# Key and value products under the list scheduler, with norm chains shared by two tiles

## The chip, the cores and the metric

The kernel runs on one core of a Trainium2 chip. The metric is device time in microseconds of one launch, as the median of several runs; the profile is one more execution with the hardware profiler on. Differences of about 0.2% (3.2 us) can be told from no change.

## The reference, cut to what matters

Two layers over x (1024 tokens, 1024 features), all in float32. Layer A is attention over a window of 128 tokens, with 16 query heads on 4 key/value heads of 64; layer B has three branches (compressed, selected and sliding window) on one shared key/value side.

```python
def swa_layer(x, ...):                     # layer A
    proj = rms_norm(x, norm_g) @ w_in      # columns: queries 1024, keys 256, values 256, gates z 1024
    q = rms_norm(q, q_gain); k = rms_norm(k, k_gain)      # per head of 64
    o = banded_attention(q, k, v, SWA_WINDOW, table, sink)
    return x + (o * silu(z)) @ w_out

def nsa_shared_kv(x, ...):                 # once, from layer A's output
    kv = rms_norm(x, norm_g) @ w_kv        # six parts of 256: cmp k, cmp v, slc k, slc v, win k, win v
    k_cmp = rms_norm(compress(kv[:, :, 0], ...), k_gain[0]); v_cmp = compress(kv[:, :, 1], ...)
    k_slc = rms_norm(kv[:, :, 2], k_gain[1]); v_slc = kv[:, :, 3]
    k_win = rms_norm(kv[:, :, 4], k_gain[2]); v_win = kv[:, :, 5]

def nsa_layer(x, ...):                     # layer B
    proj = rms_norm(x, norm_g) @ w_in      # queries 1024, branch gates 48, three gates z of 1024
    # three attentions, gated by z and the branch gates, summed, @ w_out, + x
```

`compress` takes overlapping blocks of 32 tokens (stride 16), adds a position embedding and sends each block of 32 x 64 numbers through two products with a SiLU between.

## The kernel before, in words

**Products.** The 1024 tokens are eight tiles of 128. Each float32 operand is split in a high part (rounded to TensorE's float32 format, cast by ScalarE) and a low part (the rest, a subtraction on VectorE), and a product is three: high x high, high x low, low x high. A product of a token tile with 512 columns is thus 8 x 3 matmuls (`proj_steps`, lines 291 to 293). For it the tile's rows are scaled with their norm (L333 or L335), turned on TensorE in two groups of four 128x128 blocks (L341), and split into the tensor `xt` (L228, L229).

**Norms without a square root.** The inverse root is a chain of twelve small VectorE operations (`rsqrt_steps`, L197 to L214), each on the result of the last. Each row norm of x needs one per tile, and each key tile one for its heads (`head_steps`): copy of the keys (ScalarE, L497), square (GpSimd, L447), sum (VectorE, L451), chain, product with the root (GpSimd, L465), turn (TensorE, L476), split (L231, L232), store.

**Weights.** `load_w` loads 512 KB at a time into one of two stages and splits it into a slot. Slots are a ring of seven: four in the pool `w`, three in `wx`. `preload` takes all four of `w` for weights of the attention stage, and what comes after it in the program runs on the three of `wx`.

**The order.** In layer A's keys (`layer_a`) the steps of tile i stand in lists (load, statistics and scale, turns, product, chain, turn of the keys), and `weave` interleaves the lists of successive tiles by position; the result is the order of the engines' queues (`manual_schedule`). `shared_kv` does the same with `pipeline`: first the normed rows and the first half of layer B's keys (`kv_units`, tile `bkv`), then the products for the compressed keys and values (tile `c`) and the turns of their tokens (L1216), then the compression (`hid_ck`, `hid_cv`), then the second half of the keys. Queries and gates (`query_chunk`, `z_half`) stand outside of such a region, and the framework orders them itself around it; it also fits whole regions into one another, but keeps each one's own order on every engine.

The two attention stages (`plan_a`, `plan_b`) are ordered by the class `Plan`, a list scheduler. Every operation is entered with its engine, a cost, what it comes after, the ring buffers that it opens and uses, a priority and a latency; a load also holds a modelled DMA for a time. `Plan.run` then always picks the ready operation that can start earliest,

```python
key = (max(at, free.get(e, 0.0)) + o["shy"], o["prio"], o["n"])
```

and emits it; ties go to the lower priority number. The costs are written into the program; the chip's own times don't enter.

**Gates.** Layer A's gates z (`z_half`, tile `z_a`) follow its queries: the four key loads of two halves each (`load_keys`, 512 KB each, from DRAM), then four branches of weights `az`; at branch 1 `preload` comes first. A gate's store is issued by ScalarE itself. Layer B has twelve such branches, in the order c = 0 to 3 and, inside, b = 0 to 2; there `preload` comes ahead of branch (2, 0).

## Time and profile before

| | us |
|---|---|
| median of three runs | 1600.13 (1598.68 to 1600.6) |
| the profiled execution | 1605.16 |
| its span, first to last instruction | 1603.4 |
| mean granted TensorE clock | 0.979 |

The times of the trace are microseconds from the start of the span. Layer A's keys and values are made up to about 95 us, its queries to 190, its gates to 254, its attention and output to 485; layer B's keys and compressed keys take 498 to 693, its queries to 794, its gates to 965, its attention and output the rest. PE is TensorE, DVE VectorE, ACT ScalarE, POOL GpSimd and SP SyncE, whose only work is to issue loads and stores; a q behind a name means the engine's sequencer. A clock of 0.5 is 1.2 GHz, 1.0 is 2.4 GHz.

### The profile page before, as it was taken

The numbers are of one execution on the slowest core, as the hardware profiler recorded it, in microseconds if no ns is written. First come the engines' busy times: TensorE is split into PE (matmuls) and PEld (weight loads), VectorE is DVE, ScalarE is ACT, GpSimd is POOL, SyncE is SP. The second block draws the span as 40 slices with busy tenths as digits, with TensorE's granted clock in tenths as the row PEclk, the third lists the DMA queues.
The fourth block names the chain that finished last, engine by engine and source line by source line (L and its number), as shares of the span: only waits on it lengthen the run. The fifth ranks groups of instructions, "written<-read, shape, count | busy, mean of one in ns | idle before, by whom it ended". The sixth has DMA issues, their size and how long they took to land.

```text
span 1603.4 us, 26419 instructions
## 1 busy us (share of the span) xinstructions
PE 1518.9 (95%) x8579; PEld 1206.2 (75%) x8579; DVE 981.1 (61%) x4051; ACT 786.1 (49%) x1895; POOL 344.2 (21%) x442
## 2 busy tenths in 40 slices
PE   5899998989996989999999999999999999989998
PEld 3678876767774868899888787777787787768777
DVE  6668723766535645589732434877787787576531
ACT  4323323765633334233332433877677777675530
POOL 2124300112000100133300000332333343354300
PEclk8999999999997989999999999999999999999999
DMA  5265486554325323365553443435423433363132
GB/s 188 68 178 147 128 224 184 158 185 141 103 83 180 103 76 95 111 168 130 147 148 109 131 125 112 127 86 142 115 83 117 146 99 102 112 193 91 42 114 93
DMA packets 199692, 203.89 MB, mean 127 GB/s; under 512 B 22159, under 2 KB 160098, under 8 KB 199556
## 3 DMA queue, kind: packets, MB, share of 16 engines
q1 hardware_dynamic: 177552, 189.50, 40.7%
q10 hardware_dynamic: 21124, 10.49, 2.3%
q0 software_dynamic: 880, 2.23, 0.6%
q8 instruction: 68, 1.11, 0.3%
q14 instruction: 68, 0.56, 0.1%
HBM read 147.41 MB, written 56.85 MB: 127 GB/s over the span
## 4 chain that ended last, share of the span: by engine, by line
PE 61%; DVE 4%; DMA 2%; issue 1%; ACT 1%; POOL 1%; SPq 0%; POOLq 0%; DVEq 0%; ACTq 0%
PE o_b L857 7%; PE pt_sb L848 4%; PE s_sb L1381 4%; PE z_b L320 3%; PE z_b L321 3%; PE z_b L322 3%; PE s_wb L1381 3%; PE pt_wb L848 3%; PE z_b L619 2%; PE bq L291 2%; PE bq L292 2%; PE bq L293 2%; PE z_b L620 2%; PE z_b L621 2%; PE op L759 2%; PE op L760 2%
## 5 line engine op out<-in xcount | busy, mean ns | idle before, releaser
L910 ACT ACTIVATE p_sb<-p_sb,negm_sb 128x128 f32<-128x128 f32 (+7 forms) x128 | 98.8, 774 | 10.8 <-DVE negm_sb L1418 10.1
L910 ACT ACTIVATE p_wb<-p_wb,negm_wb 128x640 f32<-128x640 f32 (+4 forms) x128 | 88.7, 695 | 22.1 <-DVE negm_wb L1418 21.3
L320 PE MATMUL z_b<-xt_b,w_bz 128*128 128x512 f32 x240 | 95.1, 398 | 3.9 <-ACT w_bz L231 3.9
L852 ACT COPY p_sb<-pt_sb 128x512 f32<-128x512 f32 x143 | 78.2, 587 | 41.9 <-PE pt_sb L848 41.5
L1381 PE MATMUL s_sb<-k,q_b 128*128 128x384 f32 (+3 forms) x384 | 96.5, 368 | 2.1 <-DVE mx_sb L1409 1.7
L321 PE MATMUL z_b<-xt_b,w_bz 128*128 128x512 f32 x240 | 94.9, 395 | 0.0
L322 PE MATMUL z_b<-xt_b,w_bz 128*128 128x512 f32 x240 | 94.8, 395 | 0.0
L568 DVE SCALAR_TENSOR_TENSOR zt_b<-zt_b,z_b 128x512 f32<-128x512 f32 x48 | 32.8, 686 | 98.1 <-ACT zt_b L565 98.0
L1381 PE MATMUL s_wb<-k,q_b 128*128 128x384 f32 (+3 forms) x384 | 85.8, 334 | 2.4 <-issue 1.7
L852 ACT COPY p_wb<-pt_wb 128x512 f32<-128x512 f32 x120 | 67.9, 583 | 36.7 <-PE pt_wb L848 35.8
L900 POOL TENSOR_TENSOR uz_b<-uz_b,rb_b 128x512 f32<-128x512 f32 x32 | 42.1, 1316 | 190.9 <-DMA rb_b<-rdb 158.2
L848 PE MATMUL pt_sb<-consts,p_sb 128*128 128x128 f32 x576 | 79.8, 276 | 1.2 <-ACT p_sb L852 0.7
L848 PEld LDWEIGHTS pt_sb<-consts,p_sb 128*128 128x128 f32 x576 | 65.4, 140 | 17.2 <-issue 10.0
L565 ACT ACTIVATE zt_b<-z_b 128x512 f32<-128x512 f32 x48 | 28.5, 596 | 96.9 <-PE z_b L322 76.4
L910 ACT ACTIVATE p_a<-p_a,negm_a 128x256 f32<-128x256 f32 (+1 forms) x128 | 61.7, 483 | 27.8 <-DVE negm_a L1109 19.9
L770 DVE TENSOR_TENSOR xo<-op,xo 128x512 f32<-128x512 f32 x32 | 22.1, 690 | 86.3 <-PE op L761 86.2
L900 POOL TENSOR_TENSOR uz_a<-uz_a,rb_a 128x256 f32<-128x256 f32 x32 | 25.0, 782 | 222.7 <-DMA rb_a<-rda 199.8
L857 PE MATMUL o_b<-p_sb,v 128*64 128x256 f32 x576 | 72.8, 391 | 0.0
L1400 DVE CUSTOM_DVE_ANT_1 p_sb<-s_sb,sel_b 128x256 f32<-128x256 f32 (+3 forms) x128 | 56.6, 453 | 25.7 <-PE s_sb L1381 21.7
L848 PE MATMUL pt_wb<-consts,p_wb 128*128 128x128 f32 x480 | 71.1, 275 | 0.1
L1558 POOL TENSOR_TENSOR pc_b<-pc_b,mxc_b 128x256 f32<-128x256 f32 x32 | 20.7, 647 | 233.1 <-DVE mxc_b L1555 186.4
L1381 PEld LDWEIGHTS s_sb<-k,q_b 128*128 128x128 f32 x384 | 62.6, 191 | 9.9 <-issue 2.9
(386 smaller groups left out, 4605.1 us busy)
## 6 DMA issues: line engine op xcount, KB each, us to landing
ws_bz<-in_b_w_in_dram SPq DMA_DIRECT2D x24, 512.0 KB
uz_b<-uzb SPq DMA_DIRECT2D x32, 384.0 KB
qda<-qs_aq SPq DMA_DIRECT2D x64, 128.0 KB
q_a<-qda SPq DMA_DIRECT2D x32, 256.0 KB
qdb<-qs_bq SPq DMA_DIRECT2D x64, 128.0 KB
q_b<-qdb SPq DMA_DIRECT2D x32, 256.0 KB
rb_b<-rdb SPq DMA_DIRECT2D x64, 128.0 KB
uzb<-zt_b ACTq DMA_DIRECT2D x30, 256.0 KB
```

What stands on the lines that cost most here:

```text
L291: mm(ps, xh, w(0, k), start=(k == 0), stop=False)
L320: mm(ps, wh, xh, start=(k == 0), stop=False)
L321: mm(ps, wl, xh, start=False, stop=False)
L322: mm(ps, wh, xl, start=False, stop=(k == KC - 1))
L568: nc.vector.scalar_tensor_tensor(c["t"], c["t"], 1.0, ps(), op0=ALU.add, op1=ALU.mult)
L848: nc.tensor.transpose(t[:, g * P : (g + 1) * P], p()[:, g, cols], self.ident)
L852: nc.scalar.copy(p()[:, :, cols], t) if e == "ACT" else nc.vector.tensor_copy(p()[:, :, cols], t)
L857: nc.tensor.matmul(o()[z * HD : (z + 1) * HD], v()[:, blocks[j], :], p()[:, z::2, j * P : (j + 1) * P], start=(j == 0), stop=(j == n - 1),)
L900: nc.gpsimd.tensor_tensor(u(), u(), c["b"], op=ALU.mult)
L910: self.nc.scalar.activation(p[:, g, :n], p[:, g, :n], AF.Exp, bias=negm[:, g : g + 1], accum_out=sums[:, g : g + 1])
L1381: nc.tensor.matmul(s["s"][:, : nbk * P], cq(g), k[:, y, (b0 + at) * P : (b0 + at + nbk) * P], start=(y == 0), stop=(y == 1),)
L1400: nc.vector.tensor_tensor_reduce(out, src, term, 1.0, NEG, ALU.add, ALU.max, acc)
```

## The change

The keys and values of layer A, and all of `shared_kv`, are entered into a `Plan` instead of lists. One plan covers layer A's loads of x, weights, norms, turns, products and keys, and the weights of the first queries. A second one covers layer B's keys, the compression and the weights of the first queries there (`w3`). Row norms of layer A share a chain in groups (0), (1), (2, 3), (4, 5), (6, 7); keys share copy buffer, square, sum, chain, turn, split and store by two tiles. In layer A rows 4 to 7 of x and two weight stages use the memory of the bias tables `dd`, and all low parts of the key weights are VectorE's (half of them were GpSimd's). Queries turn and split up to 512 columns at once. In layer A's gates SyncE keeps the program's order, and the key loads come after the last branch's weights, their first 256 columns for all heads ahead of the rest. In layer B the preload comes one branch earlier.

```diff
+    def plan_rsqrt(self, get, n, scale, name, c, after, new, use, prio):
+
+        for k, step in enumerate(self.rsqrt_steps(get, n, scale, name, c)):
+            after = [self.plan.op("DVE", 0.19, step, after, [] if k else new, use + (new if k else []), prio, 0.02)]
+        return after[0]
...
+    def plan_weights(self, w, c0, n, name, prio, gain=None, rows=D, stage=None, own=None, early=None):
...
+            part = m * n / SLOT
+            pr = prio[j] if isinstance(prio, list) else prio + 0.01 * j
+            a = plan.op("SP", 0.5, load, [], stgs, [], pr if early is None else early + 0.01 * j, 2.5, held=2.0 * part)
+            a = plan.op("ACT", part if gain is None else 0.15 * m + 0.9 * part, high, [a], ws, stgs, pr)
+            b = plan.op("DVE", 1.22 * part if gain is None else 0.1 * m + 1.25 * part, low, [a], [], stgs + ws, pr)
...
+    def plan_proj(self, c, xt, i, weights, xops, name, prio, parted=False, first=()):
...
+        if parted:
+            order = [(k, (0,)) for k in (0, 1, 2, 3)] + [(0, (1,)), (1, (1,)), (4, (0,)), (5, (0,)), (2, (1,)), (3, (1,))]
+            order += [(6, (0,)), (7, (0,))] + [(k, (1,)) for k in (4, 5, 6, 7)]
+        else:
+            order = [(k, (0, 1)) for k in range(KC)]
+        a, steps = None, []
+        for n, (k, ys) in enumerate(order):
+            need = [made[k][0] if 0 in ys else None, made[k][1] if 1 in ys else None]
+            a = plan.op(
+                "PE", 0.227 * (2 * (0 in ys) + (1 in ys)), run(k, ys, n == 0, n == len(order) - 1),
+                [a] + need + xops[k // 4] + (list(first) if n == 0 else []), [] if n else [mb],
+                bufs[k] + ([mb] if n else []), prio, 0.35 if n == len(order) - 1 else 0.0,
+            )
...
+    def plan_norm(self, c, j, x, after, xt, i, name, prio, gain=None, xbuf=()):
...
+        a = plan.op("DVE", 1.31 if gain else 0.72, scale, after, [], ([chain] if chain else []) + list(xbuf), prio)
...
+            t = plan.op("PE", 0.66, turn, [a], [tb], list(xbuf), prio + 0.1 * k)
+            b = plan.op("ACT", 0.57, high, [t], [], [tb], prio + 0.1 * k)
+            b = plan.op("DVE", 0.66, low, [b], [], [tb], prio + 0.1 * k)
...
+    def plan_keys(self, pool, cs, bufs, ready, kd, gain, m, name, prio, gop=None):
...
+        rs = [plan.op("ACT", 0.36, raw(0), [ready[0]], [kb], [bufs[0]], prio)]
+        rs.append(plan.op("ACT", 0.36, raw(1), [ready[1]] + rs, [], [kb, bufs[1]], prio))
+        a = plan.op("POOL", 1.08, square, rs, [sb], [kb], prio)
+        a = plan.op("DVE", 0.66, reduce, [a], [cb], [sb], prio)
+        a = self.plan_rsqrt(lambda: c["hs"], 8, 1.0 / HD, nm, c, [a], [], [cb], prio)
+        a = plan.op("POOL", 1.06, normed, [a], [nb], [kb, cb], prio)
+        a = plan.op("PE", 0.66, turn, [a], [tb], [nb], prio)
+        a = plan.op("ACT", 0.57, high, [a, gop], [qb], [tb], prio)
+        a = plan.op("DVE", 0.68, low, [a], [], [tb, qb], prio)
+        plan.op("SP", 0.5, store, [a], [], [qb], prio, 2.2, held=1.46)
...
# layer_a
+                plan_load(0, -100)
+                iop = plan.op("SP", 0.4, ident, [], [], [], -99, 2.2, held=0.3)
+                plan_load(1, -98)
...
+                wkv = self.plan_weights(
+                    w_in, 1024, 512, "akv", [-11.0, -4.0, -3.5, -3.0], stage=lambda j: places[j] if j >= 2 else None, early=-97.0
+                )
...
+                for i in range(2, NT):
+                    plan_load(i, 10.0 * i - 80)
+                waq = self.plan_weights(w_in, 0, 512, "aq0", 55.0)
...
+                for tiles in ((0,), (1,), (2, 3), (4, 5), (6, 7)):
+                    i0 = tiles[0]
+                    cb = plan.buf("chain")
+                    c = {"buf": cb}
+                    prio = 10.0 * i0 - 22
...
-            for h in range(NKV):
-                self.load_keys(ks[h], kd, h, 0, S)
-            for c in range(4):
-                if c == 1:
-                    self.preload(w_in, [1536 + (self.zfirst + k) * 256 for k in range(2)], None)
-                    self.lasting = 0
-                w = self.load_w(w_in, 1536 + c * 256, 256, f"az{c}")
...
+            with tc.manual_schedule(engines={mybir.EngineType.SP}):
+                for c in range(4):
+                    if c == 1:
+                        self.preload(w_in, [1536 + (self.zfirst + k) * 256 for k in range(2)], None)
+                        self.turn = self.lasting = 0
+                    w = self.load_w(w_in, 1536 + c * 256, 256, f"az{c}")
+                    if c == 3:
+                        for k0, k1 in ((0, 256), (256, S)):
+                            for h in range(NKV):
+                                self.load_keys(ks[h], kd, h, k0, k1)
...
# shared_kv
+            ld = plan.op("SP", 0.45, load, [], [xb], [], 10.0 * i - 99, 2.3, held=1.9)
+            xops[i] = self.plan_norm(c, 0, lambda c=c: c["x"], [ld], xt, i, "kv", 10.0 * i - 15, None, [xb])
...
+        branch(0, self.plan_weights(kw, 512, 512, "bkv0", -5.0, gain, early=-98.0), 0.0)
+        wc = self.plan_weights(kw, 0, 512, "ckv", 50.0, gain)
+        sw = plan.op("SP", 0.0, swap, [x for i in range(NT) for y in xops[i] for x in y], [], [], -100.0, 0.0)
...
+            steps, mb = self.plan_proj(c, xt, i, wc, xops[i], f"c_{i}", 100.0 + 10.0 * i)
+            for z, ops in enumerate(self.plan_tokens(p1, c, mb, [steps[-1], sw], es, i, 105.0 + 10.0 * i)):
+                tokens[z] += ops
...
+        branch(1, (wkv, made0 + made1, bufs0 + bufs1), 240.0, [rv["last"]])
+        w3 = self.plan_weights(w_in, 3 * 256, 304, "bq3", 290.0, lambda: self.gb)
...
# build
-                    if (c, b) == (2, 0):
+                    if (c, b) == (1, 2):
                         self.preload(w_in, [1072 + k * D + self.zfirst * 256 for k in range(2)], self.gb)
-                        self.lasting = 0
+                        self.turn = self.lasting = 0
```

## Rows read from the trace of the kernel before

**Rows 1.** The page's part 1, TensorE's line: busy us (share of the span) xinstructions.

```profile
PE 1518.9 (95%) x8579; PEld 1206.2 (75%) x8579; DVE 981.1 (61%) x4051; ACT 786.1 (49%) x1895; POOL 344.2 (21%) x442
```

**Rows 2.** The table by stretches: start:end, length, then busy time of each engine in each of these stretches of the span (us from its start), with the number of instructions, the granted TensorE clock, the DMA share and GB/s. In order: the keys of layer A (two stretches), its gates, the end of its attention and the step into layer B, the first keys of layer B, the token products for the compressed keys, the queries of layer B, and its gates.

```profile
10.00:35.00 25.00, 13.89 (x53) 10.30 (x52) 18.04 (x47) 11.90 (x18) 6.35 (x3) 0.83 0.60 200
...
35.00:89.00 54.00, 45.66 (x204) 35.44 (x203) 35.29 (x164) 17.92 (x36) 10.84 (x13) 0.92 0.18 56
...
190.00:254.00 64.00, 58.33 (x253) 47.14 (x251) 22.41 (x45) 16.11 (x25) 3.13 (x3) 0.95 0.82 221
...
462.00:500.00 38.00, 24.97 (x108) 20.18 (x107) 15.79 (x56) 9.45 (x20) 0.00 (x0) 0.83 0.41 140
...
500.00:553.00 53.00, 51.53 (x249) 41.25 (x248) 37.75 (x119) 20.49 (x42) 7.68 (x13) 0.96 0.48 139
...
553.00:625.00 72.00, 62.35 (x291) 49.22 (x289) 34.98 (x82) 26.00 (x55) 2.06 (x4) 0.93 0.24 71
...
693.00:794.00 101.00, 101.00 (x636) 92.12 (x635) 88.00 (x374) 35.51 (x87) 36.03 (x48) 1.00 0.58 145
...
794.00:980.00 186.00, 182.09 (x794) 149.35 (x793) 67.67 (x157) 60.49 (x133) 3.13 (x3) 0.98 0.46 129
```

**Rows 3.** The same table for seven shorter stretches, the columns as in rows 2.

```profile
23.10:26.70 3.60, 3.57 (x11) 2.92 (x12) 0.86 (x1) 1.53 (x2) 0.00 (x0) 0.51 0.56 212
...
34.30:40.30 6.00, 5.99 (x16) 4.86 (x17) 2.82 (x22) 0.59 (x1) 0.00 (x0) 0.50 0.00 0
...
54.00:57.40 3.40, 3.40 (x11) 2.71 (x12) 1.99 (x14) 0.82 (x3) 0.00 (x0) 0.50 0.00 0
...
244.40:248.50 4.10, 4.05 (x10) 3.19 (x11) 1.82 (x2) 0.49 (x1) 0.00 (x0) 0.50 0.91 286
...
498.50:504.50 6.00, 6.00 (x19) 4.76 (x20) 1.95 (x3) 1.17 (x2) 0.00 (x0) 0.50 0.58 232
...
570.50:576.20 5.70, 5.70 (x17) 4.75 (x18) 2.37 (x4) 2.04 (x4) 0.00 (x0) 0.50 0.32 83
...
898.30:903.90 5.60, 5.60 (x13) 4.45 (x14) 3.33 (x8) 2.97 (x8) 0.00 (x0) 0.50 0.71 187
```

**Rows 4.** The view of TensorE's waits, asked for one stretch of the span after another (0 to 89, 89 to 190, 190 to 254, 462 to 553, 553 to 625, 794 to 990 us): who waited <- for whom: us in total, times, longest us.

```profile
PE xt_a L341 <- DVE x L333: 21.7, 8, 7.2
...
PE qt_aq L476 <- DVE ks_a L232: 1.8, 1, 1.8
...
PE z_a L320 <- ACT w_az L228: 5.1, 1, 5.1
...
PE xt_kv L341 <- DVE xk L335: 13.0, 1, 13.0
...
PE kt_b L476 <- POOL qn_b L465: 6.8, 2, 6.1
...
PE z_b L320 <- ACT w_bz L231: 3.9, 1, 3.9
```

**Rows 5.** VectorE in the keys of layer A. First two rows of the timeline (start us, us, engine, line, operation, out<-in), the first and the last of the twelve operations of tile 0's chain; then rows of the groups by form of 0 to 90 us (line, engine, operation, shapes xcount | busy us, mean ns | idle before).

```profile
5.43 0.15 DVE L197 TENSOR_SCALAR rx_a<-ss_a 128x1 f32<-128x1 f32 x1 [3.90 <-ACT jk_a L360]
...
7.55 0.16 DVE L214 SCALAR_TENSOR_TENSOR ry_a<-rt_a,ry_a 128x1 f32<-128x1 f32 x1
...
L333 DVE SCALAR_TENSOR_TENSOR x<-x,rsa,gain 128x1024 f32<-128x1024 f32 x8 | 10.9, 1362 | 0.6 <-DVE rsa L363 0.3
...
L229 DVE TENSOR_TENSOR xt_a<-xt_a,xt_a 128x512 fp32r<-128x512 f32 x16 | 11.0, 690 | 14.9 <-ACT xt_a L228 14.9
...
L229 DVE TENSOR_TENSOR w_aq<-ws_aq,w_aq 128x1024 fp32r<-128x1024 f32 x4 | 4.9, 1228 | 3.0 <-ACT w_aq L228 3.0
...
L232 DVE SCALAR_TENSOR_TENSOR ks_a<-kt_a,cols,ks_a 128x256 fp32r<-128x256 f32 x5 | 2.4, 484 | 2.5 <-ACT ks_a L231 2.5
```

**Rows 6.** TensorE's timeline at the first transposes of tiles 1, 6 and 7 of layer A; in brackets its idle time before, and what ended it.

```profile
23.13 1.09 PE L341 MATMUL xt_a<-consts,x 128*128 128x128 f32 x4 [7.16 <-DVE x L333]
...
72.74 0.63 PE L341 MATMUL xt_a<-consts,x 128*128 128x128 f32 x4 [2.02 <-DVE x L333]
...
81.07 0.63 PE L341 MATMUL xt_a<-consts,x 128*128 128x128 f32 x4 [1.44 <-DVE x L333]
```

**Rows 7.** The end of layer A's gates: SyncE's timeline at the key loads, ScalarE's at the last cast of gate weights, and the table by stretches (columns as in rows 2) from 230 to 234 us.

```profile
218.78 7.00 SPq L515 DMA_DIRECT2D k_a<-kda  x8
...
243.35 1.04 ACT L228 CAST w_az<-ws_az 128x1024 fp32r<-128x1024 f32 x1 [4.46 <-DMA ws_az<-in_a_w_in_dram]
...
230.00:234.00 4.00, 4.00 (x20) 3.30 (x19) 0.00 (x0) 0.00 (x0) 0.00 (x0) 1.00 1.07 257
```

**Rows 8.** The step into layer B: timeline of ScalarE, SyncE and VectorE.

```profile
486.92 2.54 ACT L231 ACTIVATE w_bkv<-ws_bkv,cols 128x512 fp32r<-128x512 f32 x4
...
490.16 1.85 SPq L259 DMA_DIRECT2D ws_bkv<-in_kv_w_dram  x2
...
492.06 2.11 SPq L1234 DMA_DIRECT2D xk<-x1d  x4
...
497.60 0.75 DVE L335 TENSOR_SCALAR xk<-xk,r 128x1024 f32<-128x1024 f32 x1 [1.55 <-DMA xk<-x1d]
```

**Rows 9.** GpSimd's timeline at the key norm of the last tile of layer B's first keys.

```profile
569.81 0.61 POOL L465 TENSOR_TENSOR qn_b<-kr_b,ry_b 128x256 f32<-128x256 f32 x1 [5.96 <-DVE ry_b L214]
```

**Rows 10.** ScalarE's timeline in layer B's gates, at a part of the preloaded weights.

```profile
891.75 1.71 ACT L231 ACTIVATE w_pre<-ws_pre,cols 128x256 fp32r<-128x256 f32 x4 [2.17 <-PE z_b L322]
```

More of the change, by code (lines that the diff above doesn't have):

```diff
@@ L242, in slot, with load_w @@
         return self.wx.tile([P, 2, SLOT], F32R, tag="wx", name=name, bufs=self.wmore)
-    def load_w(self, w, c0, n, name, gain=None, rows=D, later=None, stage=None, low=None):
+    def load_w(self, w, c0, n, name, gain=None, rows=D):
         kk = SLOT // n
@@ L984, in layer_a @@
                 nc.vector.memset(one, 1.0)
-                square, *chain = units[0][1]
-                square()
-                for z in range(2):
-                    cols = slice(z * 512, (z + 1) * 512)
-                    ps_g = self.mm(f"gain_{z}")
-                    nc.tensor.matmul(ps_g, one, row[z], start=True, stop=True)
-                    nc.scalar.copy(gain[:, cols], ps_g)
-                turn = units[0][2]
-                for step in (*chain, later[0], turn[0], later[1], turn[1], later[2], later[3], *units[1][1]):
-                    step()
@@ L995, in layer_a, with ident @@
[L995 to L1004 removed]
+                def ident():
+                    nc.sync.dma_start(table[:, :P], a["consts"][:, :P])
@@ new lines, in masks, with gain_row, run, gain_copy @@
+                def masks():
+                    nc.sync.dma_start(table[:, P:], a["consts"][:, P:])
+                gc = {}
+                def gain_row(z):
+                    def run():
+                        gc[z] = self.mm(f"gain_{z}")
+                        nc.tensor.matmul(gc[z], one, row[z], start=True, stop=True)
+                    return run
+                def gain_copy(z):
+                    return lambda: nc.scalar.copy(gain[:, z * 512 : (z + 1) * 512], gc[z])
+                xs, loads = {}, {}
@@ new lines, in plan_compress @@
+        tb = plan.buf("tp")
+        a = plan.op("PE", 0.1, turn, [ld], [tb], [], prio - 30)
+        z = plan.op("DVE", 0.17, clear, [tokens[0]], [], [], prio - 30)
+        a = plan.op("ACT", 0.2, high, [a, z], [], [tb], prio - 30)
+        a = plan.op("DVE", 0.2, low, [a], [], [tb], prio - 30)
+        w, made, bufs = self.plan_weights(w1, 0, 256, f"{name}w", prio - 20, rows=2048)
+        pb = [plan.buf("mm") for _ in range(2)]
+        after = [a] + tokens
+        for k in range(16):
+            a = plan.op(
+                "PE", 0.74, product(k), after + list(made[k]), [] if k else pb, bufs[k] + (pb if k else []), prio,
+                0.0 if k < 15 else 0.3,
+            )
+            after = [a]
@@ L1195, in hidden, with bias, add @@
+        c["last"] = a
+        ends = []
+        for m in range(2):
+            u = {}
+            vb = plan.buf("hb")
+            def bias(m=m, u=u):
+                u["b"] = self.st.tile([P, 1], F32, tag="cb", name=f"cb_{name}_{m}")
+                nc.vector.tensor_copy(u["b"], c["ph"][m][:, 256:257])
+            def add(m=m, u=u):
+                u["h"] = hb = pool.tile([P, 256], F32, tag="hb", name=f"hb_{name}_{m}", bufs=2)
                 nc.vector.tensor_scalar(
-                    hb.rearrange("p (h m) -> p m h", h=NKV), ph[:, :256].rearrange("p (m h) -> p m h", h=NKV), b, None,
```

727 lines of the change are left out of this document (425 added, 302 removed).

## The prediction, made before the result

> **What bounds the kernel now.** I began with the page: TensorE is busy for 95% of the span [rows 1]. So only what TensorE waits for, or does at the lower clock, can be won. The reader sees where in the table by stretches [rows 2]: between 693 and 794 us TensorE has no idle time at all, and nothing that the change does to the queries there can show. Idle time (length less PE busy) stands in the two stretches of layer A's keys, 11.1 + 8.3 = 19.4 us; in layer A's gates, 5.7; at the step into layer B, 13.0 + 1.5; in the stretch after the first keys of layer B, 9.7; in layer B's gates, 3.9. With 1.8 us at the first query turn [rows 4] that is 55.0 us. The view of waits names what ended them [rows 4]: the scaled rows of a tile on VectorE (21.7 us in eight waits), the scaled row of layer B's first tile (13.0), the normed keys from GpSimd (6.8), and cast weights on ScalarE (5.1 and 3.9). Then I cut out the stretches at a granted clock of 0.5, which is 1.2 GHz instead of 2.4 [rows 3]: each lies right behind one of these waits; 34.4 us together, nearly all of it TensorE busy, so that half, 17.2 us, is lost once more. The pool that the change can draw on is 55.0 + 17.2 = 72.2 us. The rest of the span, the two attention stages, is not edited.
>
> **Keys of layer A (pool 19.4 + 6.5 slow).** The tiles' scale on VectorE ends every wait here, and the queue explains it: a tile has a chain of twelve small operations, 5.43 to 7.71 us, 2.3 us in all, and its keys another [rows 5]. Removed: three of eight row chains (five groups instead of eight tiles) and four of eight key chains, 7 x 2.3 = 16 us, and eight small copies. Added: two low parts of weights, 2 x 1.23, which were GpSimd's; key sums and low parts over 512 columns instead of two of 256. These have no row; a key low part costs between 0.48 (one of before) and 0.97 (two), and I take 0.69, the row of the other 128x512 low part; the sums, as many elements, I take at the same. VectorE's new total is 8 x 1.36 (scale) + 16 x 0.69 (low parts) + 8 x 1.23 (weights) + 5 x 2.3 + 4 x (0.69 + 2.3 + 0.69) = 58.0 us, with about 2 us of gaps 60, begun at 5.4. A tile takes TensorE 8.33 - 1.44 = 6.9 us, from the two tiles at 72.74 and 81.07 [rows 6]. So both engines need about the same; VectorE has little room.
> Tile 1, now at 23.13 us behind a wait of 7.16: VectorE needs chain, scale, two low parts, chain, scale and one weight part, 2.3 + 1.4 + 1.4 + 2.3 + 1.4 + 1.2 = 10.0, so 15.4 us, when TensorE is still in tile 0. Wait left: 0.5. Tile 2: two low parts, three weight parts, the pair's chain, scale, 1.4 + 3.7 + 2.3 + 1.4 = 8.8, so 24.2, with TensorE through tile 1 at 23. Wait left: 1 instead of 3.3. Afterwards a pair costs VectorE 2 x 1.36 + 4 x 0.69 + 2.3 + 3.7 = 11.5 against 13.8 of TensorE, but the four parts of the query weights (4.9) fall in the same 41 us; I leave 3 us. With the first weights' 0.7, 5.2 us of idle remain and, for two short slow stretches, 2.5. Gain 14.2 + 4.0 = 18. If VectorE were not the limit it would be 24; if its order slips, 9.
> The 1.8 us at the first query turn waits for a key low part on VectorE; one turn of 512 columns instead of two makes it 1 us less. The other query edits are worth nothing: TensorE covers them between 693 and 794 us [rows 2].
>
> **Gates of layer A (5.1 + 2.0 slow).** ScalarE's last cast waits 4.46 us for its load; SyncE issued the eight key loads at 218.78, ahead of that load in its program, and the DMA engines are full [rows 7]. With SyncE's order kept and the keys placed behind the last weights, that load meets a freer DMA, and the wait goes. What is queued behind: the 4 MB of keys, now in sixteen loads, at 257 GB/s 16.3 us beside the last gate products, and behind them on SyncE the query loads of the attention. The first scores need 256 columns only, which now go first. Gain 6 of 7.1; it is 0 if the stores of the gates, which share the DMA engines, hold ScalarE up instead.
> Here the Trainium skill speaks against the change: "DMA: Bandwidth & Descriptors", section Bandwidth, has DMAs batched to 1 MiB and more for three quarters of the peak, and the change makes 512 KB loads into loads of 128 and 384 KB. The row shows the engines full with several loads in flight (share 1.07, [rows 7]), which hides a cost per load; by the rule the keys would take longer and hold the gates up after all, and the sum would be that of the rival below.
>
> **Step into layer B (14.5 idle + 3.0 slow).** The rows show the order [rows 8]: ScalarE casts the first weights at 486.92, which frees a stage, so SyncE issues the next weights at 490.16 and only then, at 492.06, the rows of x; VectorE scales at 497.60, and 0.9 us later TensorE turns. In the list the first rows are SyncE's first operation, ahead of the weights, and their buffers lie where layer A's bias tables were, so they can be in place before 486. Late next are the weights: cast 486.9 to 488.3, low part 1.5 us on VectorE beside the last row chain of layer A, first product at 490. That leaves 4.5 us of wait and some 2.5 for the clock, and 2 for weights 2 and 3, whose stage frees at 490 as now. Gain 17.5 - 9 = 8.5; from 5 (rows not early) to 11.
>
> **After the first keys (9.7 idle + 2.8 slow).** The largest wait is GpSimd's key norm, which itself waited 5.96 us for VectorE [rows 9], with no product queued behind it on TensorE that could run. The list takes any product that is ready, and half the chains are gone. I leave 2.5 of idle (the turn of the last tokens, where little else is ready) and 1 of slow clock: gain 9. Bounds 4 and 12.
>
> **Gates of layer B (3.9 + 2.8 slow).** ScalarE's preload parts wait for TensorE to free a slot at 891.75 [rows 10], and the next weights queue behind them. Loaded one branch earlier, the preload takes slots that were freed a chunk before. Gain 6; 0 if the three slots left for the branches are too few a branch longer; the stretch from 794 to 980 has this one wait and no other [rows 2, 4], though its last part runs on those three.
>
> **Sum.** 18 + 1 + 6 + 8.5 + 9 + 6 = 48.5. Less 0.2 us for each of the sixteen tiles of layer B which are now ordered by listed costs, 3.2 (an estimate: the waits per tile of rows 6 are 1.4 to 2.0, and the list knows the durations): 45.3. The profiled execution took 1605.2 (span 1603.4): 1559.9. The median of the runs is 5.0 below the profiled execution, so 1555.
>
> **Rivals.**
> - VectorE is the bound of the keys after all, or the list's order is late by half of what I hope: keys of A 9, step and keys of B 5 + 4, gates 10, less 3: 25 us, 1575. For it: 60 us of VectorE against 8 x 6.9 = 55 of TensorE. Against it: work that isn't urgent (query weights, last keys) can lie behind.
> - The change doesn't do what it says for the keys: waits were for data (x and weights, 5 MB in the first stretch) and not for order. Then only the gates gain, 12: 1588. Against it: the wait of 7.16 ended with VectorE, not with a DMA.
> - The moved key loads hold the gates' stores up, and these ScalarE: gates of A gain nothing, 1561. The Trainium skill's rule above speaks for it.
> - Slower: the engines take their queues in listed order, and a pair's first tile now waits for the second one's load and square. Where the list's times are off, each tile waits. Price: the longest steady wait of now, 2.0 [rows 6], and half of the 3.4 slow us behind such a wait [rows 3], 3.7 for each of 24 tiles, 89 us, against the 55 us (25.9 + 17.5 + 12.5) of these stages now. That is 33 more, less 12 of the gates: 1621. It decides from (55 + 12) / 24 = 2.8 us a tile on.
>
> **How the numbers follow.** Forecast 0.57, its own range 1541 to 1570. First rival 0.22, second 0.06, the skill's 0.05, slower 0.07; 0.03 for gains and losses that cancel. Low end: the bounds above, 24 + 1.8 + 7 + 11 + 12 + 6.7 = 62, give 1538. High end: past the first rival, 1582. Faster by over 0.2% (3.2 us, about what a measurement here can tell) 0.89, within it 0.03, slower 0.08.
>
> **What would show it.** Right: tile 1 of layer A turned before 18 us and the keys' products done some 18 us earlier; idle between the last layer A product and the first turn of layer B under 5 us; no wait over 2 us around 560 to 570 or in either gate stage; the attention stages as long as now. Wrong: waits for VectorE's scale of 2 us per tile as before, many slow stretches in the planned stages, or ScalarE standing at a gate store while the keys load.

## The result

The changed kernel takes **1557.6 us** (median of four runs, 1552.8 to 1561.8) against 1600.4 us before (1598.7 to 1603.3, four runs of the same job): the ratio is 0.973, with a 95% interval of 0.9691 to 0.9769. Forecast was 1555, with a range of 1538 to 1582. The profiled execution took 1554.0 us (span 1552.2, mean granted clock 0.992), the one of before 1605.2. So profile against profile the gain is 51.2 us where the sum of the prediction has 45.3, and median against median it is 42.7: the forecast of the median is closer than its sum.

Each stage's end, read from TensorE's timeline (start of the stage's last or first matmul, us), gives the place of the gain. "Gain so far" is the difference between the columns.

| | before | after | gain so far | of the stage | forecast |
|---|---|---|---|---|---|
| last query product of layer A | 189.3 | 168.4 | 20.9 | 20.9 | 18 + 1 |
| first gate product of the attention | 254.8 | 230.5 | 24.3 | 3.4 | 6 |
| last output product of layer A | 485.1 | 462.0 | 23.1 | -1.2 | 0 |
| first key product of layer B | 500.3 | 465.1 | 35.2 | 12.1 | 8.5 |
| last query product of layer B | 793.1 | 748.2 | 44.9 | 9.7 | 9, less 3.2 |
| last of layer B's own gate products | 966.1 | 914.6 | 51.5 | 6.6 | 6 |
| last output product | 1598.9 | 1548.0 | 50.9 | -0.6 | 0 |

Two rows share work: the turn of layer B's first tile (1.03 us) now stands ahead of layer A's last output product. So 1.0 of the 12.1 us was moved there, and the loss of 1.2 us in the row above holds it.

TensorE's line in part 1 of the page after answers to [rows 1]. TensorE does the same 8579 matmuls in 14.8 us less, most of it the clock (worked out below); VectorE has 247 instructions and 35.4 us less.

```profile
PE 1504.1 (97%) x8579; PEld 1202.1 (77%) x8579; DVE 945.7 (61%) x3804; ACT 782.0 (50%) x1872; POOL 330.9 (21%) x416
```

The table by stretches of after, columns as in [rows 2], in the order of that group (its two token stretches are here one, 518 to 577, and the step and the first keys overlap):

```profile
10.00:35.00 25.00, 22.60 (x101) 18.24 (x102) 22.00 (x64) 17.86 (x31) 1.55 (x2) 1.00 0.61 222
35.00:75.00 40.00, 40.00 (x194) 31.80 (x193) 26.27 (x64) 13.21 (x26) 8.04 (x8) 1.00 0.27 84
168.00:231.00 63.00, 57.41 (x257) 47.01 (x256) 22.78 (x44) 15.45 (x21) 3.13 (x3) 0.98 0.79 218
440.00:478.00 38.00, 33.33 (x144) 26.30 (x143) 21.33 (x65) 13.09 (x27) 0.00 (x0) 0.91 0.41 135
465.00:518.00 53.00, 50.96 (x244) 41.67 (x245) 35.62 (x91) 23.50 (x48) 6.26 (x6) 0.94 0.49 148
518.00:577.00 59.00, 59.00 (x294) 48.79 (x292) 29.72 (x61) 25.92 (x56) 2.08 (x2) 1.00 0.26 83
650.00:748.00 98.00, 98.00 (x617) 89.15 (x616) 82.45 (x353) 35.27 (x83) 35.50 (x47) 1.00 0.59 151
748.00:932.00 184.00, 183.47 (x812) 150.62 (x811) 71.96 (x173) 62.34 (x136) 4.62 (x6) 1.00 0.49 136
```

These rows show that layer A's keys now have no idle TensorE time from 35 to 75 us and a granted clock of 1.00, where the stretches of before had 11.1 and 8.3 us idle at 0.83 and 0.92. In layer A's gates, though, the idle time is as large as before: 5.6 us of 63 against 5.7 of 64. Layer B's token products and gates are full.

TensorE's waits of after, asked for stretches (0 to 74, 74 to 168, 168 to 232, 440 to 518, 577 to 650, 748 to 945 us); the columns are those of [rows 4], and one row, the largest, is taken from each:

```profile
PE xt_a L403 <- DVE x L389: 4.9, 1, 4.9
...
PE qt_aq L540 <- POOL qn_aq L528: 3.5, 1, 3.5
...
PE z_a L719 <- DVE zt_a L668: 5.6, 1, 5.6
...
PE bkv L361 <- ACT w_bkv L310: 2.7, 1, 2.7
...
PE ckt L1557 <- POOL dup_ck L550: 1.6, 1, 1.6
...
PE z_b L719 <- DVE zt_b L668: 1.4, 1, 1.4
```

Of the eight waits for a tile's scale only the first is left, which has no product before it; the 13.0 at the step into layer B is 2.7 and has changed its cause; the 6.8 for GpSimd's key norm and the 3.9 for layer B's gate weights are gone. One wait of 5.6 us is new: a product of gates waits until VectorE has joined an earlier gate tile `zt_a`. The slow stretches of [rows 3] have become two in the edited stages, one behind this new wait and one behind the step:

```profile
229.10:235.90 6.80, 5.42 (x13) 4.27 (x14) 0.69 (x1) 0.60 (x1) 0.00 (x0) 0.50 0.53 165
464.60:471.40 6.80, 5.32 (x12) 3.85 (x13) 6.66 (x19) 2.73 (x5) 0.00 (x0) 0.50 0.64 185
```

**The tiles of layer A.** TensorE's timeline at the transposes of `xt_a` answers to [rows 6] (tiles 0 and 1, then the last two):

```profile
10.90 1.97 PE L403 MATMUL xt_a<-consts,x 128*128 128x128 f32 x8 [4.93 <-DVE x L389]
20.92 1.04 PE L403 MATMUL xt_a<-consts,x 128*128 128x128 f32 x8
...
49.50 1.03 PE L403 MATMUL xt_a<-consts,x 128*128 128x128 f32 x8
56.46 1.03 PE L403 MATMUL xt_a<-consts,x 128*128 128x128 f32 x8
```

Only the first has a bracket, an idle time before it. The last two are 7.0 us apart, the 6.9 of TensorE's own work that the prediction worked out. VectorE's groups by form from 0 to 74 us, as in [rows 5], have the low part of a tile of x, the one of a pair's keys and the pair's sum:

```profile
L412 DVE TENSOR_TENSOR xt_a<-xt_a,xt_a 128x512 fp32r<-128x512 f32 x16 | 10.5, 684 | 6.7 <-ACT xt_a L409 6.6
...
L591 DVE SCALAR_TENSOR_TENSOR ks_a<-kt_a,cols,ks_a 128x512 fp32r<-128x512 f32 x3 | 2.3, 751 | 3.9 <-ACT ks_a L588 3.9
L575 DVE TENSOR_REDUCE hs_a<-sq_a 128x8 f32<-128x512 f32 x3 | 2.0, 678 | 0.0
```

**The end of layer A's gates.** From SyncE's timeline the key loads, from ScalarE's the last cast of the weights and then the last two gate tiles, and the table by stretches from 220 to 224 us; these answer to [rows 7].

```profile
203.82 10.97 SPq L616 DMA_DIRECT2D k_a<-kda  x16
...
211.37 1.05 ACT L234 CAST w_az<-ws_az 128x1024 fp32r<-128x1024 f32 x1 [0.58 <-PE z_a L430]
...
225.43 0.60 ACT L665 ACTIVATE zt_a<-z_a 128x512 f32<-128x512 f32 x1 [10.79 <-DMA uza<-zt_a]
...
229.10 0.60 ACT L665 ACTIVATE zt_a<-z_a 128x512 f32<-128x512 f32 x1 [3.07 <-DMA uza<-zt_a]
...
220.00:224.00 4.00, 4.00 (x19) 3.34 (x18) 0.00 (x0) 0.00 (x0) 0.00 (x0) 1.00 1.06 258
```

The cast no longer waits for its load. But ScalarE stands for 10.79 us at a gate tile whose buffer (one of two) is being stored while the DMA engines are full with keys, and TensorE runs out of work behind it. In the kernel before ScalarE had stood at such a store too, beside the same keys and just ahead of the cast of [rows 7]:

```profile
238.29 0.60 ACT L565 ACTIVATE zt_a<-z_a 128x512 f32<-128x512 f32 x1 [12.33 <-DMA uza<-zt_a]
```

So the wait for the store is not new. Before, TensorE's wait ended later still, with the weights whose load stood behind the keys; now that load is out of the way, and the store ends the wait.

That the store is late beside the keys, and not by itself, is seen in the DMA queues of after (packets, MB, share of 16 engines), q1 with SyncE's transfers and q10 with ScalarE's: first from 200.2 to 202.4 us, ahead of the keys, then from 211.5 to 216 us, beside them.

```profile
q10 hardware_dynamic: 528, 0.26, 41.8%
...
q1 hardware_dynamic: 366, 1.00, 100.5%
```

The gate tile issued at 200.21 us is stored within the first stretch. Of the one issued at 211.54 us no packet moves in the second (it has no row of q10).

**The step into layer B** answers to [rows 8]: SyncE's load of the first rows, TensorE's first turn and first product, ScalarE's first cast of weights.

```profile
417.24 0.60 SPq L1468 DMA_DIRECT2D xk<-x1d  x1
...
429.61 1.03 PE L403 MATMUL xt_kv<-consts,xk 128*128 128x128 f32 x8
...
465.06 0.80 PE L361 MATMUL bkv<-w_bkv,xt_b 128*128 128x512 f32 x1 [2.69 <-ACT w_bkv L310]
...
464.29 1.33 ACT L310 ACTIVATE w_bkv<-ws_bkv,cols 128x512 fp32r<-128x512 f32 x2
```

The first tile is turned 32 us before layer A's last product, inside layer A's output stage, and what TensorE waits for at the step is the cast of the weights.

### The profile page after: what moved, and what is told of

Read it like the earlier page. It is cut to its first block, busy times and chain, and to the rows that moved or that the text cites. A ratio compares the mean times of both kernels' runs of the same rounds, so it can differ in the third digit from the quotient of the medians.

```text
span 1552.2 us, 26024 instructions
## 1 busy us (share of the span) xinstructions
PE 1504.1 (97%) x8579; PEld 1202.1 (77%) x8579; DVE 945.7 (61%) x3804; ACT 782.0 (50%) x1872; POOL 330.9 (21%) x416
## 4 chain that ended last, share of the span: by engine, by line
PE 80%; DVE 8%; DMA 6%; issue 2%; ACT 2%; POOL 1%; SPq 1%; ACTq 0%; DVEq 0%; POOLq 0%
PE o_b L957 8%; PE bkv L361 5%; PE s_sb L1634 4%; PE pt_sb L948 4%; PE s_wb L1634 3%; PE op L859 3%; PE op L861 3%; PE z_b L430 3%; PE op L860 3%; PE z_b L428 3%; PE z_b L429 3%; PE pt_wb L948 3%; PE c L361 3%; PE akv L361 2%; PE z_b L719 2%; PE z_b L721 2%
## 5 line engine op out<-in xcount | busy, mean ns | idle before, releaser
L1010 ACT ACTIVATE p_sb<-p_sb,negm_sb 128x128 f32<-128x128 f32 (+7 forms) x128 | 98.8, 774 | 10.2 <-DVE negm_sb L1671 9.3
L1010 ACT ACTIVATE p_wb<-p_wb,negm_wb 128x640 f32<-128x640 f32 (+4 forms) x128 | 88.7, 695 | 22.9 <-DVE negm_wb L1671 22.2
L430 PE MATMUL z_b<-xt_b,w_bz 128*128 128x512 f32 x240 | 93.9, 391 | 0.0
L429 PE MATMUL z_b<-xt_b,w_bz 128*128 128x512 f32 x240 | 93.8, 391 | 0.0
L428 PE MATMUL z_b<-xt_b,w_bz 128*128 128x512 f32 x240 | 93.7, 390 | 0.0
L361 PE MATMUL bkv<-w_bkv,xt_b 128*128 128x512 f32 x336 | 84.8, 405 | 3.7 <-ACT w_bkv L310 2.7
L948 PEld LDWEIGHTS pt_sb<-consts,p_sb 128*128 128x128 f32 x576 | 65.8, 141 | 17.8 <-issue 10.2
L361 PEld LDWEIGHTS bkv<-w_bkv,xt_b 128*128 128x128 f32 x336 | 63.7, 193 | 18.1 <-ACT w_bkv L310 3.1
```

Of the source, the lines that this page charges most:

```text
L361: mm(c["ps"], x, w(z, k), start=start and n == 0, stop=stop and n == len(ops) - 1)
L428: mm(ps, wh, xh, start=(k == 0), stop=False)
L429: mm(ps, wl, xh, start=False, stop=False)
L430: mm(ps, wh, xl, start=False, stop=(k == KC - 1))
L948: nc.tensor.transpose(t[:, g * P : (g + 1) * P], p()[:, g, cols], self.ident)
L1010: self.nc.scalar.activation(p[:, g, :n], p[:, g, :n], AF.Exp, bias=negm[:, g : g + 1], accum_out=sums[:, g : g + 1])
```

## The experiments

The changed kernel was run twice more, `a1_again` beside `h1`, `x5` and `b1`, and `a2_again` beside `x3_again`, `y2` and `y3`. Kernels of one job ran on one chip. `x1` to `x4` ran in a third job, without the changed kernel, so they are read by their stretches more than by their medians. In what follows, "gate stretch" is the time from the last query product of layer A to the first gate product of its attention: 65.5 us before, 62.1 after.

**All row norms and key norms with chains of their own** (tests whether fewer VectorE operations or their order made the keys faster).

```diff
-                for tiles in ((0,), (1,), (2, 3), (4, 5), (6, 7)):
+                for tiles in ((0,), (1,), (2,), (3,), (4,), (5,), (6,), (7,)):
...
+        twin = plan.buf("chain")
+        self.plan_rsqrt(lambda: c["hs"], 8, 1.0 / HD, nm + "t", {}, [a], [twin], [cb], prio)
```

> The changed kernel with a chain of its own for each of layer A's eight row norms, and a second chain of twelve operations, whose result nobody reads, beside each of the twelve key chains: VectorE has its fifteen shared chains back, about 35 us. Theory that the order made the gain: layer A's keys end at most 4 us later, layer B's first keys too, span 1552 to 1560. Rival, that the smaller work of VectorE made it: layer A's keys end 10 to 16 us later and layer B's 5 to 9 later, span 1570 to 1577.

Measured: 1560.7 us (1557.5 to 1562.9). Nobody reads the second key chain's result; it only takes VectorE's time. VectorE's part of the page and its stretch 10 to 75 us, beside the same stretch of after (48.27 us of VectorE in 127 instructions):

```profile
PE 1504.9 (97%) x8579; PEld 1202.3 (77%) x8579; DVE 961.1 (62%) x3983; ACT 780.8 (50%) x1873; POOL 332.7 (21%) x416
...
10.00:75.00 65.00, 62.13 (x281) 49.54 (x282) 51.35 (x197) 29.11 (x55) 7.83 (x9) 0.97 0.34 120
```

The last key product of layer A starts at 73.2 us as in the changed kernel (73.5), and layer B's first keys take as long (106.8 us from the first key product to the last token product, against 107.4). So the work of the shared chains is not what the keys gained by. What is left is the order, with what came beside it: sharing by two tiles, and memory that lets rows 4 to 7 of x be loaded earlier. No run takes these back in layer A. VectorE's timeline of the kernel before shows the order at work, at the end of tile 6:

```profile
78.18 0.69 DVE L229 TENSOR_TENSOR xt_a<-xt_a,xt_a 128x512 fp32r<-128x512 f32 x1 [1.43 <-ACT xt_a L228]
...
79.64 1.28 DVE L333 SCALAR_TENSOR_TENSOR x<-x,rsa,gain 128x1024 f32<-128x1024 f32 x1
```

The row of tile 7 was there and its chain begun at 73.16. But the chain's last operations and the scale (79.64) stand in the queue behind a low part of tile 6, for which VectorE waits 1.43 us, and TensorE then waits 1.44 us for that scale [rows 6]. What the sharing is worth shows behind the keys: from the last key product to the last query product 100.9 us instead of 94.9, with a new wait of 2.6 us for a key norm (the changed kernel's other two profiles have 93.6 and 97.4, so this is worth 3 to 7 us). An extra chain cost VectorE 15.4 / 15 = 1.0 us of busy time, not the 2.3 that it lasts, so the run gives back 15 us of work and not the 35 that were expected.

**Layer B with the lists of before**, layer A and the preload as changed (`shared_kv` and the queries replaced by those of the kernel before).

```diff
-            w3 = self.shared_kv(xt, p1, w_in)
+            self.shared_kv_old(xt, p1)
...
-                pipeline(self.query_chunk(p1, xt, w_in, cs, qd, "bq", self.gb, self.bq, *((gates, w3) if cs == (3,) else ())))
+                pipeline(self.query_chunk_old(p1, xt, w_in, cs, qd, "bq", self.gb, self.bq, gates if cs == (3,) else None))
```

> Layer A as in the changed kernel; layer B's first keys, second keys and queries have the steps of before in the pipelines of before; the gate preload stays at (1,2). Theory (the order of the list made layer B's gain): layer A as in the changed kernel (last key product at 73 to 75 us, last query product at 168 to 171, last output product at about 462), then the wait of some 13 us at the step comes back (first key product of B 15 us after the last output product instead of 3), and from there to the last query product of B 328 us as before where the changed kernel has 319 (first key product 465.1 to 748.2 is 283, before 500.3 to 793.1 is 293); in sum 20 to 23 us more: about 1579 in the median. Rival (layer B gained because its x rows and weights come at another time relative to the stores of layer A, and order matters little): 5 to 10 us more, about 1565.

Measured: 1572.3 us (1569.9 to 1574.7) against 1553.2 for the changed kernel in the same job: 19.1 more, where 20 to 23 were expected. TensorE's waits from 440 to 600 us and the two slow stretches there:

```profile
PE xt_kv L1695 <- DVE xk L1689: 13.1, 1, 13.1
PE kt_b L1725 <- POOL qn_b L528: 8.1, 3, 6.1
...
463.50:477.10 13.60, 5.18 (x16) 4.27 (x17) 5.75 (x12) 2.51 (x4) 0.00 (x0) 0.50 0.73 270
538.60:548.80 10.20, 5.45 (x16) 4.58 (x17) 5.62 (x17) 2.74 (x6) 0.61 (x1) 0.50 0.33 97
```

Both waits of [rows 4] are back, the longest ones with their old sizes (13.0 and 6.1). Last output product to first key product: 15.3 us (3.1 in `a1_again`); from there to the last query product 291.9 (282.9). That is 12.2 + 9.0, the two gains of layer B, so the list of operations is their cause. The run also takes back the sharing by two tiles; for the chains `x4` shows that this is worth nothing in the first keys, for copies, turns and stores it was not tried apart.

**Preload back at its old branch.**

```diff
-                    if (c, b) == (1, 2):
+                    if (c, b) == (2, 0):
```

> The changed kernel with layer B's preload back ahead of branch (2, 0). If the earlier place is what freed layer B's gates: one wait of about 3.9 us for cast gate weights and a slow stretch behind it come back, the gates last 6 to 7 us longer, span 1558 to 1560 against 1552. If the gates gained from how layer B's keys leave the slots, the wait stays away and the span stays at 1552.

Measured: 1559.4 us (1558.5 to 1564.7). TensorE's waits from 752 to 930 us have the old row again,

```profile
PE z_b L428 <- ACT w_bz L237: 3.9, 1, 3.9
```

with 3.4 us of slow clock behind it. Layer B's gates take 172.6 us, as before (173.0), where the changed kernel has 166.4, and the twelve profiles with the early preload lie between 165.6 and 167.1. So this edit of one line is worth 6.2 us within the changed kernel. The profiled span is 1562.5, where 1558 to 1560 were expected; 4.3 us of its difference to the 1552.2 of the changed kernel arose ahead of these gates.

**The keys loaded ahead of the gates**, in eight loads of 512 KB, with SyncE's order left to the framework.

```diff
-            with tc.manual_schedule(engines={mybir.EngineType.SP}):
+            for h in range(NKV):
+                self.load_keys(ks[h], kd, h, 0, S)
+            with ExitStack():
...
-                    if c == 3:
-                        for k0, k1 in ((0, 256), (256, S)):
-                            for h in range(NKV):
-                                self.load_keys(ks[h], kd, h, k0, k1)
```

> The changed kernel with layer A's key loads back ahead of the gates, eight of 512 KB, and SyncE's order free there. Theory: the place of the 4 MB only moves the wait (from a cast that waits for its weights to a gate that waits for its store), so the wait of 5.6 us at the end of the gates goes, one of about 5 us inside them comes back, and the span changes by 0 to 3 us: 1552 to 1555. Rival: the move was worth the 6 us of the prediction and the wait at the end has another cause: 1558 or more, with the wait at the end still there.

Measured: 1564.3 us (1560.7 to 1569.2), and a gate stretch of 68.0 us against 62.1. So placement, size and SyncE's order together are worth about 6 us; they were not separated, and 68.0 is also more than the 65.5 of before. Neither reading was quite right: the wait at the end went (1.4 us) and one inside came, as the theory had it, but at the rival's price. ScalarE's timeline, and TensorE's wait inside the gates:

```profile
211.97 0.60 ACT L665 ACTIVATE zt_a<-z_a 128x512 f32<-128x512 f32 x1 [12.01 <-DMA uza<-zt_a]
...
PE z_a L428 <- ACT w_az L234: 8.0, 1, 8.0
```

Here too ScalarE stands at a gate tile being stored beside the keys, 12.01 us. The cast of weights that TensorE wants is queued behind it, and then waits 3.41 us more for its own load.

**Three buffers for the gate tiles of layer A.**

```diff
-            c["t"] = pool.tile([P, 512], F32, tag=tag, name=f"zt_{name}_{h}", bufs=2)
+            c["t"] = pool.tile([P, 512], F32, tag=tag, name=f"zt_{name}_{h}", bufs=bufs)
...
-                            self.z_half(pz, xt, w, z, uz[c, :, :, z, :], half, f"a{c}{z}")
+                            self.z_half(pz, xt, w, z, uz[c, :, :, z, :], half, f"a{c}{z}", "zq", 3)
```

> The changed kernel with three instead of two buffers for layer A's gate outputs. Theory: ScalarE stands 10.8 us for the store that frees a gate buffer while the keys load; with a third buffer the wait of 5.6 us ahead of the attention's first product and the slow stretch behind it shrink to 0 to 2 us: span 1544 to 1547. Rival: the stores wait in their issue (ScalarE's queue waits for an earlier DMA's semaphore), and a buffer more changes nothing: 1552.

> Three gate buffers once more, in the same job as the changed kernel. Theory (the wait at the end of the gates is for the stores): the wait falls from 4 to 6 us to about 1.5, and the time by 4 to 7 us. If the difference to the changed kernel is under 2 us, the 11 us of the first time were the chip's and not the buffer's.

Measured: 1546.3 us (1543.8 to 1553.7) the first time and 1549.8 (1547.3 to 1553.5) the second, beside this one:

> The changed kernel once more, beside the next three on one chip, since single executions lay between 1552 and 1562 and single small effects are of that size: 1552 to 1558 in the median. The wait ahead of the attention's first gate product comes again, 4 to 6 us.

The changed kernel measured 1558.8 (1556.9 to 1563.6) there, nine more than the second, with no overlap. Against the kernel before the ratios of that job are 0.9684 (0.9666 to 0.9701) with three buffers and 0.9742 (0.9723 to 0.9762) without. ScalarE's timeline at the last two gate tiles and TensorE's wait, second run:

```profile
223.21 0.60 ACT L665 ACTIVATE zt_a<-z_a 128x512 f32<-128x512 f32 x1 [5.97 <-PE z_a L430]
227.51 0.60 ACT L665 ACTIVATE zt_a<-z_a 128x512 f32<-128x512 f32 x1 [3.71 <-PE z_a L430]
...
PE z_a L719 <- DVE zt_a L668: 1.4, 1, 1.4
```

ScalarE waits for products now, and the gate stretch is 57.9 us in both runs, 4.2 under the 62.1. In both runs the slow stretch behind the wait is gone as well. This shows that the wait at the end of the changed kernel's gates was for the store of a gate tile. What it is worth in the median is less sure: the first profiled span was 1551.8, where 1544 to 1547 were expected, and the next experiment bears on the nine.

**Keys in two parts**, the second issued after the last gate product in SyncE's program; with two buffers and with three.

```diff
-                        for k0, k1 in ((0, 256), (256, S)):
-                            for h in range(NKV):
-                                self.load_keys(ks[h], kd, h, k0, k1)
+                        for h in range(NKV):
+                            self.load_keys(ks[h], kd, h, 0, 256)
...
+                for h in range(NKV):
+                    self.load_keys(ks[h], kd, h, 256, S)
```

> Only the first 256 columns of the keys (eight loads of 128 KB) stay behind the last gate weights; the other eight loads, 3 MB, are issued after the last gate product, two buffers as in the changed kernel. Theory (the 4 MB of keys hold the gates' stores up): the wait at the end of the gates falls under 1.5 us with two buffers as well, 4 to 7 us less. Rival 1 (the stores are late for their own sake): the wait stays at 4 to 6. Rival 2 (the 3 MB then stand ahead of the attention's query and weight loads): the wait moves to the first scores, no gain or up to 5 us more.

> Keys in two parts as in the last kernel, and three gate buffers. If one cause is behind both, the two gains don't add up: within 2 us of the better one alone. If they do add up, 8 us and more below the changed kernel.

Measured: 1555.0 us (1550.3 to 1562.1) with two buffers, 1552.3 (1545.4 to 1556.3) with three. The edit did not do what it was meant to. SyncE's timeline and ScalarE's, with two buffers:

```profile
204.37 11.39 SPq L616 DMA_DIRECT2D k_a<-kda  x16
...
225.88 0.60 ACT L665 ACTIVATE zt_a<-z_a 128x512 f32<-128x512 f32 x1 [10.68 <-DMA uza<-zt_a]
```

All sixteen loads are issued in one go as before: SyncE waits for no product, so a place later in its program is no time later. The edit changed nothing that the rivals turn on, the gate stretches are those of two and of three buffers (61.5 and 58.5), and what a later load of the keys would do was not tried. Against rival 1 stand the rows of q10 above: ahead of the keys a store is quick. The run has one other use: in their traces every engine of `y2` has the same instructions in the same order as in `a2_again`, and `y3` as `x3_again`; yet the medians differ by 3.8 and 2.5 us. So the four are two kernels with nine runs each, medians 1556.9 with two buffers and 1550.5 with three, 6.3 us apart, and the runs overlap (1550.3 to 1563.6 and 1545.4 to 1556.3).

**The bias tables behind both query chunks**, alone and with three gate buffers.

```diff
-                for h in cs:
-                    t = dd[h]
...
+            for h in range(NKV):
+                t = dd[h]
```

> The four loads of layer A's bias tables and their additions on VectorE go behind both query chunks. Theory (VectorE stands at the first table's load for 5.3 us and holds up the query chain behind it): the 3.45 us wait at 97.7 goes, 3 us less, 1554. Rival (the tables then come late for the attention, beside the key loads and the gate weights): the wait moves into the gates, 0 or up to 5 more.

> Three gate buffers in layer A and the tables behind both query chunks. Theory: both gains add up, 11 us (three buffers) and 3 us (tables), about 1543. Rival: the tables' 1 MB falls beside the weights and keys of the gates and eats the buffers' gain: 1550 or more.

> The changed kernel once more, on the chip of the other three: 1552 to 1562 as in the four runs shown. If its times fall into two groups, 1553 and 1561, the trace of a second execution should show where the 8 us go.

Measured: 1555.1 us (1552.8 to 1555.9) alone, 1551.4 (1551.1 to 1552.0) with the buffers, and 1553.2 (1552.1 to 1554.1) for the changed kernel beside them. The tables are worth nothing that can be told: the wait at the first query turn is 2.4 us with them moved, and in the three profiles of the changed kernel it is 3.5, 2.0 and 3.6. With the tables late in both, the three buffers gained 3.7 us here (1555.1 to 1551.4), against 9.0 or 6.3 in the other job; both edits together gained 1.8, where 14 were expected, so the number of the rival (1550 or more) came. Their own stretch agrees in all jobs (57.9 to 59.1 us with three buffers, 60.8 to 62.1 with two in the changed kernel's three profiles); the rest of the difference is scatter in layer A, told next.

**The scatter of the changed kernel.** Its profiles of 1550.3 and 1558.7 us of span (`a1_again`, `a2_again`) part in layer A: last query product 166.5 and 172.2, last output product 458.7 and 468.9. From layer B's first key product to the last output product they take 1084.2 and 1082.4. The longer one has 17.0 us of slow clock in layer A instead of 6.8; two of its three slow stretches are these, behind its waits at the first query turn and at the gates (table by stretches, `a2_again`):

```profile
101.70:108.50 6.80, 5.94 (x19) 4.87 (x19) 6.08 (x20) 1.86 (x3) 3.52 (x4) 0.50 0.18 43
231.40:238.20 6.80, 4.09 (x10) 3.26 (x11) 0.69 (x1) 0.60 (x1) 0.00 (x0) 0.50 0.74 221
```

Half of the 10.2 us more at the lower clock is 5.1, and TensorE is idle for 5.3 us more of layer A (25.8 against 20.5); together about the 10.2 us by which the two ends of layer A differ. So layer A still has a few short waits of changing length, and a median of the changed kernel moves by some 5 us from job to job. The 3.2 us named at the start are too fine for such a comparison; single effects are read from their own stretch.

## Why the prediction was right, and where not

**The bound.** The pool of idle and slow time in TensorE was the right thing to count. Over the span TensorE's idle time (span less PE busy) fell from 84.5 to 48.1 us and its busy time by 14.8: 36.4 + 14.8 = 51.2. Of its busy time 43.6 us lay at the lower clock before and 21.0 after; half of the difference, 11.3, is what the clock gave back, and the other 3.5 us of busy time stay open. Only busy time may be counted so: at the step into layer B of before 11.0 us of the 17.1 slow ones are idle.

**Keys of layer A: 18 + 1 forecast, 20.9 measured at the last query product.** The mechanism holds, the balance does not. The step "both engines need about the same; VectorE has little room" put 58.0 us of work on VectorE; from 5.4 to 75 us of after it is busy for 50.8, without the keys of the last pair (3.7 in the sum). It was tight from 10 to 35 us (22.0 of 25) and had room from 35 to 75 (26.3 of 40), where TensorE has no idle time. Low parts and sums came out as taken (0.68 to 0.75 against 0.69). The oversized term is the chain: 2.3 us were entered as VectorE time, and `x4` puts an extra chain at 1.0, which leaves room for other operations in between. For the same reason "seven chains less" was the wrong cause; `x4` restores their work and the keys end at the same time. "If VectorE were not the limit it would be 24" was the case that came: the last key product starts 22.2 earlier (95.7 to 73.5). The term of 1 us at the first query turn had the wrong sign: that wait was 1.8 us for VectorE and is 3.5 for GpSimd's normed queries, so that 20.9 of the 22.2 are left. The sign "tile 1 turned before 18 us" failed (20.92) although the wait was gone: TensorE was still in tile 0, and VectorE's scale of tile 1 ended at 18.9, not at 15.4. The first rival (VectorE the bound) falls with `x4`. The second (waits for data and not for order) falls by its price, no gain in the keys; at the end of tile 6 the trace of before shows the order, but what the earlier loads gave was not tried apart.

**Gates of layer A: 6 forecast, 3.4 measured.** The step that failed is "that load meets a freer DMA, and the wait goes". The cast's wait did go (4.46 to 0.58 of idle). What is late next, the stores of the gates, was named only as a way to fail, though ScalarE's timeline of before already had it: 12.33 us at a gate store, just ahead of the cast that was read. The third rival and the last of the wrong signs had this mechanism, but not by the move: the store stands beside the keys in either place (12.33 us before, 10.79 after, 12.01 in `x2`). The rival's price, no gain, did not come; the wait of 5.6 us and the slow stretch of 6.8 took back the 4.2 us of the stretch that `x3` regains with a buffer. The Trainium skill's "DMA: Bandwidth & Descriptors", section Bandwidth, which has larger DMAs reach more of the peak, was weighed in the prediction as the ground of that rival. The traces don't bear this ground out: with sixteen loads of 128 and 384 KB the stretch 220 to 224 us moves 258 GB/s at a share of 1.06, with eight of 512 KB it was 257 at 1.07 [rows 7]. What a store stands beside is a queue of 4 MB, in loads of either size.

**Step into layer B: 8.5 forecast, 12.1 measured.** The working had the first rows early and the weights late, and that is the trace. The waits left were put at 4.5 + 2 us, and are 2.7 + 1.0 + 1.0. Mis-sized is "first product at 490", 5 us behind the last product of layer A: it is 3.1 behind it, as the row is already turned at 429.61. The row of the table ends at the first product, though, while the 8.5 also counts what comes behind it; up to the first product the working has 10.3 us (500.3 to 490).

**After the first keys: 9 forecast, 9.7 measured**, and the 3.2 us "for each of the sixteen listed tiles" were not lost: between 518 and 577 us and between 650 and 748 TensorE has no idle time. By `h1` the gain is the list's: 9.0 us come back with the old lists.

**Gates of layer B: 6 forecast, 6.6 measured, 6.2 by undoing it.** The bound "0 if three slots are too few a branch longer" didn't come in.

**The slower rival** (a pair's tile waits for the second one) has nothing for it: no wait for a tile's scale is left but the first.

**The sum.** Four of five terms came out larger by 0.6 to 3.6 us and the deduction was empty, against 2.6 too much in the gates and 1.8 lost in the attention stages (1.0 of it the turn moved there): 51 instead of 45. That makes 5.9 us too much in the forecast of the profiled execution (1559.9 against 1554.0). The step to the median erred the other way: the 5.0 that the median of before lies below its profiled execution were taken over, and the median of after lies 3.6 above its own. So the good fit of 1555 to 1557.6 is luck in part: two errors that nearly cancel.

## What to carry to other kernels

Where an engine's idle time sits behind small chains, look first for ready work that the order keeps behind them: giving back fifteen chains moved the end of these keys by nothing, while giving back layer B's old lists, tile by tile, cost 19 us. Before moving a load out of the way of one wait, read what the waiting engine stood at just before: here it was a store beside the same loads, which the move left in place. One more buffer for the stored tile (three instead of two) was worth 4 us in the stretch. An instruction's place in a queue says when it is issued only if that queue waits for something.

## What had not been expected of the hardware

A store of 256 KB that stands beside the key loads holds its buffer long: issued at 211.54 us, it released ScalarE at 225.43, 13.9 us later, while the DMA engines were at a share of 1.06; ahead of the keys one of the same size was through 2.2 us after its issue. And a chain of twelve dependent operations that lasts 2.3 us took only 1.0 us of VectorE's busy time when it was added beside other work.
